# GpSimd's tables for the second layer, issued behind a gate in the first MLP

## The chip, the cores and the metric

The kernel runs on one core of a Trainium2 chip. The core has five engines that run side by side, each with its own in-order queue: TensorE (PE, with its weight loads as PEld), VectorE (DVE), ScalarE (ACT), GpSimd (POOL) and SyncE (SP), which here only issues DMAs. The metric is the device time of one execution in microseconds (us), the median of several runs. All data is float32.

## The reference

Two decoder layers on a residual of 512 tokens by 1024 channels. Each layer projects the normed residual once, feeds three mixers (sparse attention, an S5 state space, a Mamba-2 SSD), projects their outputs back, and then applies an MLP of width 4096:

```python
for l in range(DEPTH):                      # DEPTH = 2
    h = _rmsnorm(x, norm_mix_g[l])
    z = h @ w_in[l]
    q, k, v, qi, ki, wi, u5, z_ssd, xbc, dt_raw = _split(z, IN_SIZES)
    attn_out = _dsa_mixer(q, k, v, qi, ki, wi, attn_q_norm_g[l], ..., cos, sin)
    s5_out = _s5_mixer(u5, s5_lambda_re[l], s5_lambda_im[l], s5_log_step[l],
                       s5_b_re[l], s5_b_im[l], s5_c_re[l], s5_c_im[l], ...)
    ssd_out = _ssd_mixer(z_ssd, xbc, dt_raw, ...)
    mix = jnp.concatenate([attn_out, s5_out, ssd_out], axis=-1) @ w_out[l]
    x = x + mix
    h2 = _rmsnorm(x, norm_mlp_g[l])
    x = x + ((jax.nn.relu(h2 @ w_up[l]) ** 2) @ w_down[l])
```

What the change moves are tables that depend on parameters alone and not on x: for S5 the discretised input matrices, their powers, the rotations of each chunk and a short convolution kernel, and for attention the rotary tables with the gains of the norms folded in. The set for the second layer can be made at any time before that layer's mixers read it.

## The kernel before

**Matrix products.** Every large product runs as three matmuls of hi and lo parts (lines 436 to 438, psum tile `pm`). The class `Slabs` brings the weights: a slab of 128 x 512 is loaded by SP (`wraw`), its high part `whi` is made by ACT (L171), and its low part `wlo` by DVE (L172). Slabs are requested and split three and one ahead in the code, with 3 buffers for `wraw` and 5 for `whi` and `wlo`.

**Stages.** A layer is `mixers(l)` and then `mlp(l)`. The mixers are some eight generators (the W_in slices, keys, top-k selection L1076 and L1077, attention, S5, SSD, the out projection) that `merge` traces side by side. The MLP walks four quarters of the hidden width, each as four pairs of up tiles (relu squared: ACT L1381, DVE L1384, ACT L1385, DVE L1386) and four pairs of down tiles (DVE L1392, and L1393 into the residual `x`).

**Tables.** `s5_tables(l)` makes S5's tables. For the second layer all its elementwise work is on POOL: `bb` (L589 to L594), the products in the helper `outer` (L604 to L606) for `s5b`, `BPp` and later `CA`, the rotations `COS` and `SIN` (L630 to L640), a sign on `s5bc` (L645), and for the convolution kernel `strip` (L660, L661) and a cleared `M` (L663). Between them PE transposes `BPp` (`s5B`, L618) and multiplies `CA` (`s5st`, L653), and SP copies `strip` into `M` (L666). `rope_tables(l)` makes `ropec`, `ropeq`, `ropes` and `ropeg` on POOL (L955 to L966). For the first layer both stand in the mixers; for the second they are the generator `prepare(1)`, which `run` merges with `mlp(0)`, so in the text they come during the first MLP.

**What sets the order.** The text is not the order. A scheduler takes every traced instruction with a priority (its place in the trace) and with what it depends on, and puts on each engine's queue, in its own model of time, the most urgent instruction that is ready. The second layer's tables depend on nothing late, so on POOL, which has little else to do, they are taken as soon as their buffers are free, long before their place in the text; what needs a buffer of the mixers (`ropec`) or a PE result (`CA` onward) comes later.

Of the kernel before, what the change touches and what calls it, by code (L numbers as in the profile page):

```python
# [21 lines left out]
L = 2  # L22
NB = S // P          # token blocks
KC = D // P          # channel chunks of the trunk
# [8 lines left out]
T5 = 8               # tokens of one S5 chunk  # L33
C5 = S // T5         # S5 chunks
G5 = 16
GBUFS = {"g": 52, "t": 16}
BANKS = {"m": 4, "a": 4}    # PSUM banks: trunk, attention, S5 and SSD
EARLY = 2           # slabs loaded along with x
S5_ON_DVE = True
CONV_ON_ACT = False  # L40
# how the streams of work of a layer's mixers are laid side by side: the order of W_in's slices, the blocks whose
# selections run side by side, the parts of the out projection, which of S5 and SSD waits for the other, each
# stream's pace and delay, and the banks
# [41 lines left out]
WB = (3, 5)    # weight slabs in flight: as loaded, and split  # L85
OUTER = {"tok": True, "chan": True}    # products slab by slab
AHEAD = (3, 1)    # slabs requested and split ahead of the one in use

# columns of the packed per-partition parameters
# [18 lines left out]
# constants  # L108
# [8 lines left out]
# W_in slices: (first column, width), in the host's column order  # L117
# [17 lines left out]
class Slabs:  # L135
    """slabs of weight matrices in the order of their use: loaded and split into hi and lo parts some way ahead"""
# [9 lines left out]
    def turn(self, key):  # L146
        """whether the slabs before these have been used up"""
        return self.i == self.starts[key]
# [32 lines left out]
    def take(self, n, tiles, outer):  # L181
        """the next n slabs for each of some tiles, as (tile, slab number, hi, lo): slab by slab if outer, else
        tile by tile, and then those to follow are split while the last tile uses these up"""
        if outer:
            for j in range(n):
                hi, lo = self.next()[0]
                for t in range(tiles):
                    yield t, j, hi, lo
            return
        cur = []  # L190
        for t in range(tiles):
            for j in range(n):
                if t == 0:
                    cur += self.next()
                elif t == tiles - 1:
                    self.load(self.i + AHEAD[0] + j)
                    self.split(self.i + AHEAD[1] + j)
                yield t, j, cur[j][0], cur[j][1]


class Net:
    def __init__(self, ctx, tc, a, taps=None):
# [11 lines left out]
        self.uid = 0  # L214

# [9 lines left out]
    def h(self, shape=(P, 512), dt=F32, name="h"):  # L225
        """as g, for S5 and SSD"""
        return self.g(shape, dt, name, "h")

    def tt(self, shape=(P, 512), dt=F32, name="t"):
        """as g, for the matrices of S5"""  # L230
        return self.g(shape, dt, name, "t")

    def small(self, n, tag="g"):
        """[P, n] tiles for what one stretch of small instructions needs, cut from one slot"""
# [59 lines left out]
    def rsqrt(self, y, x, n, eng=None):  # L294
        """y = 1/sqrt(x), [P, n] small"""
# [11 lines left out]
    def stt(self, v, out, x, s, y, op0, op1):  # L307
        """out = (x op0 s) op1 y, [P, n] small; GpSimd takes two instructions for it"""
# [7 lines left out]
    def expacc(self, out, x, t, v):  # L316
        """out = exp(x) to about an ulp, [P, n] small"""
# [15 lines left out]
    def sincos(self, c, s, th, t, v):  # L333
        """c, s = cos(th), sin(th), [P, n] small"""
# [14 lines left out]
        self.stt(v, q, q, 1.0, r, ALU.add, ALU.mult)      # sin(th/2)  # L349
# [4 lines left out]
        # cos(th/2) = 1 + w  # L354
# [9 lines left out]
    def norm_chunk(self, c, squares=True):  # L364
        """hi and lo parts of x*g, and the sum of squares over channels (still per partition)"""
# [25 lines left out]
    def token_sums(self, acc, perm=False):  # L391
        """[P, 4]: mean square + eps per token; block b is tokens b*128 + m, or with perm 4m + 3-b"""
# [10 lines left out]
    def bcast_tokens(self, colv, k):  # L403
        """[P, 4] per-token columns -> psum tile [P, 512] with the token's value on every partition"""
# [6 lines left out]
    def add_slabs(self, l):  # L411
        """the weights of a layer, in the order of their use"""
# [20 lines left out]
    def mm3(self, p, lh, ll, rh, rl, first, last):  # L433
        """p += (lh+ll)^T (rh+rl), without the product of the two low parts (below float32's last bit)"""
# [5 lines left out]
    def gemm_tok(self, ps, xh, xl, slabs, sls):  # L440
        """token-major blocks: psum tile of block i [tok, n] = ps(i), tokens sls[i]; yields (cost, finished tile)"""
# [14 lines left out]
    def gemm_chan(self, ps, slabs, xh, xl):  # L456
        """channel-major tiles of 128 columns of a slice of 256: [chan, tok]; yields (cost, finished tile)"""
# [13 lines left out]
    def s5_small(self):  # L471
        """powers of the discretised state matrix and the input matrices, both layers"""
# [38 lines left out]
        # powers 0..8  # L511
# [17 lines left out]
        # X = (pr; pi), Y = (-pi; pr) on the two halves of the partitions  # L529
# [8 lines left out]
        # m8 and the rotation of one chunk, with the angle's sign turned on the lower half  # L538
# [4 lines left out]
        self.rot = []          # e^{+-i phi 2^k}  # L543
# [22 lines left out]
    def s5_tables(self, l, t):  # L566
        """the matrices of one layer's chunked recurrence, into t"""
# [29 lines left out]
        def outer(v, out, u, w, u2, w2, gs, d0, d1):  # L597
            """out[g, d, h] = u[g, h] w[g, d] + u2[g, h] w2[g, d]"""
# [9 lines left out]
        for q in range(4):  # L608
# [4 lines left out]
            BPp = self.tt([P, 4, 8, 16], name="BPp")               # d = 1..8: the states stand one step ahead  # L613
            outer(v, BPp, bbr, X, bbi, Y, gs, 1, 9)
            # transposed input powers: rows (d, h')
# [8 lines left out]
        # rotations by chunk  # L624
# [21 lines left out]
        for q in range(4):  # L646
            v = eng(f"C{q}")
            gs = slice(4 * q, 4 * q + 4)
            ca = self.tt([P, 4, 8, 16], name="CA")                 # d = 0..7
# [7 lines left out]
            # the skip term joins the kernel's first tap  # L657
# [14 lines left out]
    def s5(self, l, tab, usb, out):  # L672
        """usb: token-major input -> hi/lo of the two channel-major output tiles"""
# [5 lines left out]
        # input with rows (d = 7-i, h')  # L679
# [48 lines left out]
        # rows (half of the groups, chunk)  # L728
# [16 lines left out]
        # channel-major, columns (token of the chunk, half, chunk)  # L745
        gg = []
        for jh in range(2):
# [8 lines left out]
            v.scalar_tensor_tensor(t, t, 1.0, p, ALU.add, ALU.mult)      # 2 gelu(y)  # L756
# [25 lines left out]
    def ssd(self, l, r_, out):  # L782
# [3 lines left out]
        # step sizes  # L786
# [37 lines left out]
        # convolution and silu, each with half the argument  # L824
        xc = {}
        for m in (0, 1, 2, 3) if self.plan["w_order"].index("xa") < self.plan["w_order"].index("xb") else (2, 3, 0, 1):
# [16 lines left out]
            else:  # L843
                # C of each group, with zeros on the other group's partitions
# [8 lines left out]
        for b in range(NB):  # L853
            bs = slice(b * P, (b + 1) * P)
            # the sums of a dt up to each token of the block, on every partition
# [10 lines left out]
            # token-major inputs  # L866
# [12 lines left out]
            # scores  # L879
# [33 lines left out]
        # gate and group norm  # L913
# [30 lines left out]
    def rope_tables(self, l):  # L944
        """gains folded into the rotation, c and s for (k, k, ki) and for the rotated part of q; the gains of the rest of
        q stand in those of k"""
        nc = self.nc
        v = nc.gpsimd
        cos = self.tab_("cos").rearrange("p (b e) -> p b e", b=NB)     # (cos | cos)
        sin = self.tab_("sin").rearrange("p (b e) -> p b e", b=NB)     # (-sin | sin)  # L950
# [18 lines left out]
    def head_ms(self, out, src, nh):  # L969
        """mean square over the 64 of each head, + eps"""  # L970
# [6 lines left out]
    def rope(self, x, rs, c, s):  # L977
        """x = rope(x * rs * gain), of the keys"""
# [8 lines left out]
    def rope_q(self, x, c, s):  # L987
        """the rotated part of eight heads' queries"""
# [8 lines left out]
    def attn_keys(self, l, ksb, rt):  # L997
        """ksb: [P, 3, 64] per block (k0 k1 ki): norm, rope, transposes"""
# [7 lines left out]
        # hi and lo parts of the keys, each on both halves of the partitions  # L1006
# [18 lines left out]
    def transpose_heads(self, src):  # L1025
        """[P, 8, 64] token-major -> per head [P (hi d, lo d), P tokens]"""
# [15 lines left out]
    def head_dot(self, p, q, K, i, nk):  # L1042
        """p[tok, key] = q . k, both with all of their bits"""
# [3 lines left out]
    def index_scores(self, b, qi, K, wi, accs):  # L1047
        """masked scores of block b (>= 1): [P, (b+1)*128]"""
# [21 lines left out]
    def topk_masks(self, accs):  # L1070
        """the 128 largest of each row (lowest index first among equals) keep 0, the rest get NEG"""
# [10 lines left out]
    def attend(self, b, qT, K, mask, nrs, ah, al):  # L1082
        """nrs: minus the scale of each head's logits"""
# [42 lines left out]
    def merge(self, name, streams):  # L1126
        """trace several streams of work side by side: in a given order, or each at its own pace"""
# [4 lines left out]
        def step(i):  # L1132
            if i not in live:
                return True
            self.tc.cur_priority -= prio[i]
            try:
                c = next(gens[i])
# [7 lines left out]
        while live:  # L1145
            for i in sorted(live, key=lambda i: clock[i]):
# [6 lines left out]
                # blocked: it resumes no earlier than the others stand  # L1153
# [3 lines left out]
    def trunk_in(self, l, r):  # L1157
        """the slices of W_in"""
# [17 lines left out]
        def done(k, i, p):  # L1176
            """the finished tile i of a slice out of its bank"""
            if k == "u5":
                if "usb" not in r:
                    # S5 input, tokens 8c + 4e + 3-b at row (c, e) of block b  # L1180
# [7 lines left out]
            elif k[0] in "xz":  # L1188
                # SSD inputs, channel-major
# [11 lines left out]
            else:  # L1201
# [6 lines left out]
                else:  # L1208
                    t = self.g([P, NH, 64], name=k)            # the queries in pairs (r, 4+r)
# [11 lines left out]
        if l == 0:  # L1221
            # the first two slices side by side, as the channels of x come in
# [27 lines left out]
        for k in order:  # L1250
# [7 lines left out]
            else:  # L1258
                # every key of the first block is kept: no scores
# [81 lines left out]
    def out_proj(self, l, mix, part):  # L1341
        """x += (the chunks of some of the mixers) @ (their rows of w_out)"""
# [19 lines left out]
    def mlp(self, l):  # L1362
# [10 lines left out]
        nc.scalar.activation(rb, self.bcast_tokens(r2, "a"), AF.Copy)  # L1373
        for q, up, j in plan:
# [27 lines left out]
    def prepare(self, l):  # L1402
        """what the next layer's mixers need of their parameters"""
# [22 lines left out]
    def run(self, stop=None):  # L1426
        self.tc.cur_priority = 100000
        self.load()
        for l in range(L):
# [6 lines left out]
            if l + 1 < L:  # L1436
                streams.append((self.prepare(l + 1), 0.0))
# [96 lines left out]
```

## Time and profile before

| | us |
|---|---|
| runs | 1361.53, 1359.96, 1359.14 |
| median | 1359.96 |
| span of the profiled execution | 1356.7 |
| PE busy | 1247.9 (92%) |
| DVE busy | 883.2 (65%) |
| ACT busy | 564.6 (42%) |
| POOL busy | 161.6 (12%) |

All stretches below are in us from the start of the span. The first layer's mixers run to about 362, the first MLP follows up to some 600 us, and then the second layer's stages. L12 is line 12 of the kernel before. POOL's own busy time is small over the whole, and most of it lies in the first 250 us. A row of the timeline gives the start, the duration, what ran, and in brackets how long the engine had been idle and what released it. A row of the windows gives a stretch, its length, and for each engine the busy time and the number of instructions. A duration includes any time in which the instruction, once begun, is held up.

### The profile page before, as it was taken

How to read it: one execution, taken by the hardware profiler on the slowest of the kernel's cores; microseconds unless marked ns; L12 is line 12 of the kernel's file. 1: busy time of each engine (PE TensorE's matmuls, PEld its weight loads, DVE VectorE, ACT ScalarE, POOL GpSimd, SP SyncE). 2: the span in 40 equal slices, each digit the busy share in tenths (PEclk: the TensorE clock that was granted, in tenths of full speed). 3: DMA queues.
4: the chain of work that ended last, by engine and by line, in shares of the span. 5: the costliest groups of instructions: out<-in, count | busy, mean ns of one | idle time of the engine just before them, and what ended most of it. 6: DMA issues, size and time to landing. Idle time of an engine off the chain costs nothing. (4 is left out here: it accounts for less than half of the span.)

```text
span 1356.7 us, 17071 instructions
## 1 busy us (share of the span) xinstructions
PE 1247.9 (92%) x5852; PEld 1013.6 (75%) x5852; DVE 883.2 (65%) x2044; ACT 564.6 (42%) x1160; POOL 161.6 (12%) x301
## 2 busy tenths in 40 slices
PE   6679966879999999999999998978999999999998
PEld 5667854647888877888888897755688888888887
DVE  6899799884844544444466779998575444445443
ACT  4346352563542332423444535656454233242331
POOL 2593268200000221000000000000000000000000
PEclk9789987899999999999999998989999999999999
DMA  6122120001233323323323312100123333333332
GB/s 193 47 78 71 25 68 11 32 1 47 86 95 100 94 83 94 101 96 99 94 84 89 100 31 53 63 16 16 35 83 102 95 99 94 101 94 101 93 108 86
DMA packets 102694, 103.74 MB, mean 76 GB/s; under 512 B 10960, under 2 KB 95696, under 8 KB 102608
## 3 DMA queue, kind: packets, MB, share of 16 engines
q1 hardware_dynamic: 102608, 102.66, 25.1%
q8 instruction: 46, 0.75, 0.2%
q14 instruction: 40, 0.33, 0.1%
HBM read 99.36 MB, written 2.10 MB: 75 GB/s over the span
## 5 line engine op out<-in xcount | busy, mean ns | idle before, releaser
L172 DVE TENSOR_TENSOR wlo<-wraw,whi 128x512 fp32r<-128x512 f32 (+1 forms) x368 | 253.8, 691 | 300.6 <-ACT whi L171 298.4
L171 ACT ACTIVATE whi<-wraw 128x512 fp32r<-128x512 f32 (+1 forms) x368 | 229.0, 624 | 498.5 <-PE pm L437 332.4
L436 PE MATMUL pm<-xh,whi 128*128 128x512 f32 x608 | 239.8, 395 | 2.7 <-ACT usb L1186 1.1
L437 PE MATMUL pm<-xl,whi 128*128 128x512 f32 x608 | 238.5, 393 | 0.0
L438 PE MATMUL pm<-xh,wlo 128*128 128x512 f32 x608 | 238.4, 393 | 0.0
L438 PE MATMUL pm<-uh,wlo 128*128 128x512 f32 x512 | 199.5, 390 | 1.2 <-DVE wlo L172 1.2
L437 PE MATMUL pm<-ul,whi 128*128 128x512 f32 x512 | 199.7, 390 | 0.0
L436 PE MATMUL pm<-uh,whi 128*128 128x512 f32 x512 | 199.6, 390 | 0.0
L436 PEld LDWEIGHTS pm<-xh,whi 128*128 128x128 f32 x608 | 115.2, 190 | 27.6 <-ACT q L1210 1.6
L438 PEld LDWEIGHTS pm<-xh,wlo 128*128 128x128 f32 x608 | 115.1, 189 | 24.4 <-issue 0.3
L437 PEld LDWEIGHTS pm<-xl,whi 128*128 128x128 f32 x608 | 115.3, 190 | 23.1 <-DVE xl L372 0.2
L438 PEld LDWEIGHTS pm<-uh,wlo 128*128 128x128 f32 x512 | 96.2, 188 | 21.7 <-DVE wlo L172 1.6
L436 PE MATMUL pm<-whi,xh 128*128 128x512 f32 (+2 forms) x240 | 94.1, 395 | 19.8 <-ACT xh L370 12.4
L437 PEld LDWEIGHTS pm<-ul,whi 128*128 128x128 f32 x512 | 96.2, 188 | 20.3 <-issue 0.4
L436 PEld LDWEIGHTS pm<-uh,whi 128*128 128x128 f32 x512 | 96.2, 188 | 19.9 <-issue 0.2
L437 PE MATMUL pm<-wlo,xh 128*128 128x512 f32 (+2 forms) x240 | 92.5, 386 | 2.3 <-DVE wlo L172 2.3
L438 PE MATMUL pm<-whi,xl 128*128 128x512 f32 (+2 forms) x240 | 92.2, 388 | 1.5 <-DVE xl L372 1.4
L436 PEld LDWEIGHTS pm<-whi,xh 128*128 128x128 f32 x240 | 55.9, 234 | 27.1 <-ACT xh L370 12.8
L437 PEld LDWEIGHTS pm<-wlo,xh 128*128 128x128 f32 x240 | 56.3, 235 | 7.6 <-DVE wlo L172 3.4
L438 PEld LDWEIGHTS pm<-whi,xl 128*128 128x128 f32 x240 | 55.7, 234 | 7.1 <-DVE xl L372 2.5
L1384 DVE SCALAR_TENSOR_TENSOR ur<-pm,ur 128x512 f32<-128x512 f32 x64 | 44.0, 687 | 25.5 <-ACT ur L1381 25.5
L1392 DVE TENSOR_TENSOR sq<-pm,r2b 128x512 f32<-128x512 f32 x64 | 44.2, 690 | 23.2 <-PE pm L438 23.2
(349 smaller groups left out, 1915.2 us busy)
## 6 DMA issues: line engine op xcount, KB each, us to landing
wraw<-in_w_up_dram SPq DMA_DIRECT2D x128, 256.0 KB, 2.7
wraw<-in_w_down_dram SPq DMA_DIRECT2D x128, 256.0 KB, 2.7
wraw<-in_w_in_dram SPq DMA_DIRECT2D x64, 256.0 KB, 2.7
wraw<-in_w_out_dram SPq DMA_DIRECT2D x32, 256.0 KB, 2.7
wraw<-in_w_in_dram SPq DMA_DIRECT2D x16, 166.0 KB, 2.3
x<-in_xT_dram SPq DMA_DIRECT2D x8, 256.0 KB, 5.9
out_dram<-x SPq DMA_DIRECT2D x8, 256.0 KB, 2.0
s5bc<-in_s5bc_dram SPq DMA_DIRECT2D x4, 256.0 KB, 4.7
```

What stands on the lines that cost most here:

```text
L171: nc.scalar.activation(hi, raw, AF.Copy)
L172: nc.vector.tensor_tensor(lo, raw, hi.bitcast(F32), ALU.subtract)
L436: nc.tensor.matmul(p, lh, rh, start=first, stop=False)
L437: nc.tensor.matmul(p, lh, rl, start=False, stop=False)
L438: nc.tensor.matmul(p, ll, rh, start=False, stop=last)
L1384: v.scalar_tensor_tensor(r, p, 0.0, r, ALU.max, ALU.mult)
L1392: v.tensor_tensor(t, d[1], rb, ALU.mult)
```

## The change

`mlp(0)` now also issues one small POOL copy, the gate, of `r2`, which is the reciprocal of the norm's mean square that opens the MLP (L1371 before). Each step of `prepare(1)` is traced under `issue_after` the gate: POOL instructions that it traces may not be put ahead of the gate in POOL's queue. Nothing is removed, and apart from the copy nothing is added; the work on other engines that `prepare(1)` traces keeps its place.

```diff
         r2 = self.s([P, 4], tag="r2", bufs=1)
         v.reciprocal(r2, ms)
         rb = self.g(name="r2b")
         nc.scalar.activation(rb, self.bcast_tokens(r2, "a"), AF.Copy)
+        if l + 1 < L:
+            self.gate = nc.gpsimd.tensor_copy(self.s([P, 4], tag="gate", bufs=1), r2)
         for q, up, j in plan:
...
             self.tc.cur_priority -= prio[i]
+            held = len(streams[i]) > 2 and streams[i][2] == "prep"
             try:
-                c = next(gens[i])
+                with self.tc.issue_after(self.gate.ins) if held and self.gate else nullcontext():
+                    c = next(gens[i])
...
             if l + 1 < L:
-                streams.append((self.prepare(l + 1), 0.0))
+                streams.append((self.prepare(l + 1), 0.0, "prep"))
```

The orders of DVE, ACT and SP are those of before, and PE's too but for two neighbouring matmuls late in the program; only POOL's changes. In the rows below names are as in the program, a number behind a name is the scheduler's count of buffers, and lines of the kernel after stand one higher up to L966 and a few higher behind.

The first place is POOL in the middle of the first mixers, at 111 to 137 us of the trace, where it makes the first layer's `CA`. Before:

```order
L605 TENSOR_TENSOR pt_1669<-s5bc_109,s5Y 128x512
L660 TENSOR_TENSOR pt_1680<-cons,s5dd_112 16x64
L606 TENSOR_TENSOR CA_1668<-CA_1668,pt_1669 128x512
L605 TENSOR_TENSOR pt_1780<-s5bc_109,s5Y 128x512
L965 TENSOR_TENSOR ropes_5055<-cols,rows 128x4x8
L966 TENSOR_TENSOR ropes_5055<-cols,rows 128x4x8
```

After:

```order
L606 TENSOR_TENSOR pt_1669<-s5bc_109,s5Y 128x512
L661 TENSOR_TENSOR pt_1680<-cons,s5dd_112 16x64
L607 TENSOR_TENSOR CA_1668<-CA_1668,pt_1669 128x512
L606 TENSOR_TENSOR pt_1780<-s5bc_109,s5Y 128x512
L664 MEMSET M_399_1683 128x512
L605 TENSOR_TENSOR CA_1779<-s5bc_109,s5X 128x512
```

Before, the second layer's rope tables (eight rows of `ropes` and one of `ropeq`) stand ahead of the first layer's next `M` and `CA`; now these follow at once, and the rope rows stand behind the gate.

The second place is POOL where the first layer's tables end and the second layer's begin, at 175 to 193 us of the trace. Before (`CA_2145`, `M_507` and `strip_2155` are the last of the first layer; `bb_4590`, `s5b_1109` and `BPp_4604` belong to the second):

```order
L604 TENSOR_TENSOR CA_2145<-s5bc_109,s5X 128x512
L606 TENSOR_TENSOR CA_2145<-CA_2145,pt_2146 128x512
L590 TENSOR_TENSOR pt_4591<-s5bc_4584,s5ci 128x256
L645 TENSOR_SCALAR s5bc_4585<-s5bc_4585,cols 128x512
L663 MEMSET M_507_2160 128x512
L589 TENSOR_TENSOR bb_4590<-s5bc_4584,s5cr 128x256
L661 TENSOR_TENSOR strip_2155<-strip_2155,pt_2157 16x4x16
L593 TENSOR_TENSOR bb_4590<-s5bc_4584,s5cr 128x256
L591 TENSOR_TENSOR bb_4590<-bb_4590,pt_4591 128x256
L594 TENSOR_TENSOR pt_4595<-s5bc_4584,s5ci 128x256
L604 TENSOR_TENSOR s5b_1109_4599<-bb_4590,s5X 128x64
L604 TENSOR_TENSOR BPp_4604<-bb_4590,s5X 128x512
```

After:

```order
L605 TENSOR_TENSOR CA_2145<-s5bc_109,s5X 128x512
L607 TENSOR_TENSOR CA_2145<-CA_2145,pt_2146 128x512
L664 MEMSET M_507_2160 128x512
L662 TENSOR_TENSOR strip_2155<-strip_2155,pt_2157 16x4x16
L1379 COPY gate_3598<-r_885_3589 128x4
L590 TENSOR_TENSOR bb_4592<-s5bc_4586,s5cr 128x256
L591 TENSOR_TENSOR pt_4593<-s5bc_4586,s5ci 128x256
L594 TENSOR_TENSOR bb_4592<-s5bc_4586,s5cr 128x256
L592 TENSOR_TENSOR bb_4592<-bb_4592,pt_4593 128x256
L595 TENSOR_TENSOR pt_4597<-s5bc_4586,s5ci 128x256
L605 TENSOR_TENSOR s5b_1110_4601<-bb_4592,s5X 128x64
L605 TENSOR_TENSOR BPp_4606<-bb_4592,s5X 128x512
```

The second layer's tables ran straight on from the first layer's and between them; now the gate stands between the two, and everything behind it waits for the reciprocal in the MLP. From the first `COS` of the second layer onward POOL's order is the same in both.

## Rows read from the trace of the kernel before

**Rows 1.** The page: busy time, share and instructions of each engine.

```profile
PE 1247.9 (92%) x5852; PEld 1013.6 (75%) x5852; DVE 883.2 (65%) x2044; ACT 564.6 (42%) x1160; POOL 161.6 (12%) x301
```

**Rows 2.** Windows: start:end, length, PE, PEld, DVE, ACT, POOL, PEclk, DMA share, GB/s.

```profile
190.00:246.00 56.00, 34.24 (x165) 26.23 (x163) 53.59 (x103) 15.87 (x32) 51.62 (x105) 0.82 0.07 19
380.00:440.00 60.00, 60.00 (x266) 49.74 (x265) 28.41 (x43) 18.76 (x32) 0.83 (x3) 1.00 0.32 97
439.00:449.00 10.00, 10.00 (x46) 8.29 (x45) 7.12 (x8) 2.53 (x4) 8.83 (x17) 1.00 0.34 104
```

**Rows 3.** Timeline of PE in the first mixers: start, us, what, idle before and releaser.

```profile
194.54 0.47 PE L739 MATMUL s5y<-CA,X 128*64 128x128 f32 x2 [4.23 <-DVE X L726]
...
206.73 0.48 PE L739 MATMUL s5y<-CA,X 128*64 128x128 f32 x1 [6.72 <-DVE X L726]
```

**Rows 4.** Timeline of DVE in the same stretch, S5's chunk rotations and scans.

```profile
184.92 1.98 DVE L720 TENSOR_TENSOR_SCAN sw<-s5m,sv 128x64 f32<-128x64 f32 x8
...
189.45 2.65 DVE L716 TENSOR_TENSOR sv<-sv,svs 128x512 f32<-128x512 f32 x1
192.02 2.46 DVE L726 TENSOR_TENSOR X<-sw,sws 128x504 f32<-128x504 f32 x1
194.41 5.66 DVE L720 TENSOR_TENSOR_SCAN sw<-s5m,sv 128x64 f32<-128x64 f32 x8
...
201.47 1.52 DVE L724 TENSOR_TENSOR sw<-sw,COS 128x512 f32<-128x512 f32 x1
...
203.00 1.45 DVE L725 TENSOR_TENSOR sws<-sws,SIN 128x512 f32<-128x512 f32 x1
204.37 1.72 DVE L1107 TENSOR_SCALAR pe<-pe,psum 128x128 f32<-128x128 f32 x3
```

**Rows 5.** Same DVE lines where POOL is idle: second layer (ns min/median/max), one earlier.

```profile
L716 DVE TENSOR_TENSOR sv<-sv,svs x2: 682/684/685, 827.7 to 833.8; 128x512 f32<-128x512 f32 x2
...
L726 DVE TENSOR_TENSOR X<-sw,sws x2: 675/676/678, 834.4 to 839.7; 128x504 f32<-128x504 f32 x2
...
L724 DVE TENSOR_TENSOR sw<-sw,COS x2: 692/692/693, 832.6 to 837.9; 128x512 f32<-128x512 f32 x2
...
L725 DVE TENSOR_TENSOR sws<-sws,SIN x2: 684/684/685, 833.2 to 838.5; 128x512 f32<-128x512 f32 x2
...
155.58 0.67 DVE L1107 TENSOR_SCALAR pe<-pe,psum 128x128 f32<-128x128 f32 x3
```

**Rows 6.** POOL's timeline around the first and the second layer's tables.

```profile
132.30 0.25 POOL L965 TENSOR_TENSOR ropes<-cols,rows 128x32 f32<-128x32 f32 x1 [20.53 <-DVE rsw L993]
...
181.70 2.35 POOL L645 TENSOR_SCALAR s5bc<-s5bc,cols 128x512 f32<-128x512 f32 x1 [7.59 <-DMA s5bc<-in_s5bc_dram]
...
190.26 0.71 POOL L591 TENSOR_TENSOR bb<-bb,pt 128x256 f32<-128x256 f32 x1
...
213.04 0.12 POOL L630 MEMSET COS<- 128x8 f32 x1
...
439.17 0.25 POOL L961 TENSOR_TENSOR ropec<-cols,rows 128x32 f32<-128x32 f32 x1 [192.35 <-PE pm L438]
...
482.45 1.06 POOL L604 TENSOR_TENSOR CA<-s5bc,s5X 128x512 f32<-128x512 f32 x1 [34.45 <-PE s5B L618]
```

**Rows 7.** Later DVE lines beside POOL's tables, 189 to 248, then line 1033 later.

```profile
L769 DVE SCALAR_TENSOR_TENSOR sig<-sig,ge x4: 405/632/837, 223.8 to 228.0; 128x256 f32<-128x256 f32 x4
...
L1033 DVE TENSOR_TENSOR hhl<-q,hhl x2: 937/958/979, 243.5 to 246.2; 128x256 fp32r<-128x256 f32 x2
...
L1033 DVE TENSOR_TENSOR hhl<-q,hhl x8: 400/418/426, 866.7 to 937.0; 128x256 fp32r<-128x256 f32 x8
```

**Rows 8.** The first MLP: its opening norm, a slab's low part, and that line beside POOL.

```profile
362.58 0.17 DVE L1371 RECIPROCAL r<-ms 128x4 f32<-128x4 f32 x1
...
375.01 0.69 DVE L172 TENSOR_TENSOR wlo<-wraw,whi 128x512 fp32r<-128x512 f32 x1 [2.03 <-ACT whi L171]
...
L172 DVE TENSOR_TENSOR wlo<-wraw,whi 128x512 fp32r<-128x512 f32 x4 | 3.8, 944 | 3.6 <-ACT whi L171 3.6
```

More of the change, by code (lines that the diff above doesn't have):

```diff
@@ L1 @@
 import math
-from contextlib import ExitStack
+from contextlib import ExitStack, nullcontext
 import numpy as np
@@ L214, in __init__ @@
         self.uid = 0
+        self.gate = None
     def nm(self, s):
```

## The prediction, made before the changed kernel ran

> **What bounds the kernel now.** I read the page first. PE is busy 92% of the span and POOL 12% [rows 1], so over the whole, PE is the bound and POOL cannot matter. That average hides the stage that the change touches, so I read the windows next [rows 2]. From 190 to 246 us, in the first mixers, DVE is busy 53.59 of 56 us, PE only 34.24, at a granted clock of 0.82, and POOL 51.62. There DVE is the bound. From 380 to 440 us, in the first MLP, PE is busy 60.00 of 60 us at full clock, DVE needs 28.41, and POOL is idle. There PE is the bound and DVE has half its time free.
>
> Then PE's timeline in the first stretch: PE stands 4.23 and 6.72 us, both times until DVE has written `X` [rows 3]. So what DVE does just before those two instants sets the end of the stage. DVE's timeline shows what: single instructions of 1.45 to 5.66 us [rows 4]. The same forms in the second layer, where POOL does nothing, take 0.68 us [rows 5]. And POOL's timeline shows what runs beside them: from 181.70 us on, its instructions follow one another until 439.17 - 192.35 = 246.82 us [rows 6], and by the names in the order from about 185 on nearly all are the second layer's tables.
>
> **What the change takes away: DVE's slowed instructions.** I go through the slowed ones in order, each against the same form without POOL [rows 4, 5]; for the eight scans I take the eight just before, 1.98 us.
> - L716: 2.65 - 0.68 = 1.97
> - L726: 2.46 - 0.67 = 1.79
> - eight of L720: 5.66 - 1.98 = 3.68
> - L724: 1.52 - 0.69 = 0.83
> - L725: 1.45 - 0.68 = 0.77
> - three of L1107: 1.72 - 0.67 = 1.05
>
> The sum is 10.1 us. It lies between 189.45 and 204.37 + 1.72 = 206.09 us, a stretch of 16.6 us; so without POOL the same work takes 6.5 us, and DVE ran here at 6.5 / 16.6 = 39% of its speed. All of it stands ahead of an `X` on which PE waits, so it should come off the path whole, as long as nothing else is late by less than 10 us.
>
> After 206 us POOL goes on, with smaller instructions. The two groups that I can price: four of L769 at a mean of 632 ns where the fastest took 405, 0.9 us; two of L1033 at 958 where the second layer has 418, 1.1 us [rows 7]. That is 2.0 us more, 12.1 in all. I take 11: the first 10.1 and about half of the rest, since between 206 and 246 the work also passes through PE and ACT and not every instruction of DVE is waited for. The 80 or so DVE instructions there that I did not price may hold as much again as the 2.0, so the upper end of the gain is 14.6 with the 0.5 below.
>
> A rule of the Trainium skill names a cause. The page "SBUF — State Buffer", section "Who interferes with whom", says that VectorE and GpSimd share one pair of ports under an exclusive lock: whoever issues first has it for the whole instruction and the other stands, where the VectorE instruction has two inputs in SBUF and the GpSimd one reads SBUF. Nearly all the forms slowed above fit it in kind, but not in size: read as one lock for each instruction, L716 would lose at most one POOL instruction, about 0.71 us [rows 6], and it lost 1.97. By that reading the six lines above would hold some 0.7 us for each of 15 instructions at most, which is 10.5, and the sum would stay. The same section speaks against the change: the lock goes with the work to wherever the tables are made, and VectorE's `wlo` also has two SBUF inputs.
>
> **What it moves: the tables into the MLP.** Behind the gate POOL has 246.82 - 181.70 = 65 us of tables and a few us of rope rows, starting when the reciprocal is done, at 362.58 us [rows 8] in before's time. DVE will be slowed there. It needs 28.41 of 60 us, 47% [rows 2]. The wide instructions of the tables, which slowed it to 39%, last from 181.70 to 213.04 us [rows 6], 31 us. In those 31 us DVE falls behind by (0.47 - 0.39) x 31 = 2.4 us, and then catches up. Against that stands its lead: `whi` and `wlo` have five buffers, one in use and four ahead; a slab feeds 12 matmuls at 60.00 / 266 = 0.226 us each [rows 2], so four slabs are 10.8 us, less the 0.69 of a `wlo` and about as much for its `whi`: 9.5 us. DVE's idle time before a `wlo` ends with ACT's `whi` [rows 8], so DVE itself is not late now. The direct evidence is the one place where POOL already works in the MLP: from 439 to 449 us POOL is busy 8.83 of 10 us, `wlo` takes 944 ns on average in place of 690, and PE is busy 10.00 of 10 [rows 2, 8]. I take a cost of 0, by that row, and keep 0 to 2.4 as its bounds.
>
> **The wait that it adds.** The gate stands in POOL's queue, and behind it stand only the second layer's tables, then `ropec` and `CA`. Who waits for these: `ropec` got its buffer at 439.17, and `CA` waited 34.45 us for PE's `s5B` until 482.45 [rows 6]. Tables made from 363 on are done at about 363 + 65 + 4 = 432, 7 us before the first and 50 before the second. `s5B` stands in PE's queue where it stood, and so do the DMAs of `s5bc` and of `strip` in SP's: a DMA that waits for tables finds them done. Nothing is queued behind the gate that the first layer needs; its last `M` and `strip` now stand just ahead of it. The copy itself is 128 x 4 and lies in POOL's free time: 0.
>
> **What it moves for the first layer.** `ropes` kept POOL standing for 20.53 us until 132.30 [rows 6], waiting for DVE to release it, with the first layer's `CA` behind. These go up to 20 us earlier. PE is not shown waiting for them, and where they overlap DVE they slow it earlier by as much as they now slow it later: I take 0, with 0.5 either way.
>
> **The sum.** 11.0 + 0 - 0 = 11.0 off the profiled span of 1356.7, so 1345.7. The median of the runs, 1359.96, lies 3.3 above that span; the same on top gives **1349.0**.
>
> **Rivals.**
> - *Part of the gain is caught by another wait.* Ahead of the same matmuls stand ACT's evictions and the `strip` DMAs, and behind 206 us a chain through PE and ACT. If these are late by half, 3 to 8 us are left, 5.5 in the middle: 1354.5. For it: PE runs there at 0.82 of its clock and is itself busy 34 of 56 us [rows 2]. Against it: both waits of PE name DVE's `X`, and DVE is busy 96% of the stretch.
> - *Nothing happens.* DVE's slow instructions would be slow for another reason than POOL, or the MLP takes back what the mixers give: 1360. For it: I argue from overlap alone. Against it: the second layer runs the same forms, on the same shapes, at a quarter of the time.
> - *Slower: POOL keeps DVE out in the MLP.* The mechanism is the same slowing, in the stage where PE is the bound. At no progress at all for 65 us DVE would fall back by 0.47 x 65 = 31 us; 9.5 are covered, 21 land on PE, less the 11 won: 1370. It decides from the point where 9.5 + 11 = 20.5 of the 31 us are lost, a progress of DVE of 16% of full speed throughout. The worst single row is 0.68 of 2.65, 26% [rows 4, 5], and a slowed DVE has 53% of its time to spare.
>
> By the skill's rule read literally, the MLP's instructions from PSUM (L1384, L1392) would not be touched and only those with two SBUF inputs would; the backlog would be smaller than the 2.4 above, and the time the same 1349.0.
>
> **How the numbers follow.** Forecast, a gain of 9 to 14.6: 0.64, with 0.02 above that. Part of it: 0.22. Nothing: 0.07. Slower: 0.05. 0.2% of the median is 2.7 us, about what a measurement of this kernel can tell from no change; the first two cases lie beyond it. So faster is 0.88, same 0.07, slower 0.05. The low end is 1360.0 - 14.6 = 1345.4. The high end goes into the second case as far as a gain of 4.5, 1355.5: that leaves out a third of that case, both others and the 0.02, some 2 in 10.
>
> **What would show it.** In the profile after: POOL idle from about 175 us to the MLP, then busy some 65 us; the lines of rows 4 at 0.68 us, or 2 us for eight scans, between 185 and 200; PE's two waits for `X` gone or under 2 us; the MLP beginning about 11 us earlier; `wlo` at 0.9 to 1.5 us in the first part of the MLP with PE still busy 60 of 60. The prediction is wrong in its first step if those lines are fast and the MLP begins no earlier (another wait came due), and in its second if PE stands before L438 or L436 for `wlo` in the MLP. If `s5B` or `ropec` is late, POOL took far longer than 65 us beside DVE.

## The result, and the profile after

The changed kernel took 1345.42 us (median of 1344.43 to 1347.79) against 1359.55 us for the kernel before, of which there are four runs now: a ratio of 0.9897, 95% interval 0.9882 to 0.9912, so 14.1 us less. Run four times more, against 21 runs of the kernel before, it took 1347.55 us, ratio 0.9905 (0.9892 to 0.9919). The prediction was 1349.0 us in a range of 1345.4 to 1355.5: a gain of 11, where 12 to 14 came.

The windows of the first mixers and of the first MLP after the change (start:end, length, PE, PEld, DVE, ACT, POOL, PEclk, DMA share, GB/s):

```profile
190.00:246.00 56.00, 40.54 (x214) 30.48 (x213) 52.44 (x142) 25.00 (x61) 0.00 (x0) 0.85 0.12 37
...
360.00:420.00 60.00, 60.00 (x266) 49.73 (x265) 38.51 (x46) 20.30 (x34) 54.28 (x104) 1.00 0.31 97
```

Against [rows 2]: POOL does nothing any more in this stretch of the first mixers, where it was busy 51.62 us, and DVE does more in the same 56 us, 142 instructions for 103. In the MLP POOL is now busy 54.28 of 60 us, DVE is busy 38.51 us with 46 instructions, where 46 took 30.30 us from 374 to 434 us before the change, and PE is still busy 60.00 of 60.

PE's two waits for `X` are nearly gone (timeline: start, us, what, idle before and releaser), against 4.23 and 6.72 us in [rows 3]. The third row is what follows on `s5y`:

```profile
190.90 0.43 PE L740 MATMUL s5y<-CA,X 128*64 128x128 f32 x2 [0.18 <-DVE X L727]
...
196.31 0.32 PE L740 MATMUL s5y<-CA,X 128*64 128x128 f32 x1 [1.48 <-DVE X L727]
...
200.28 1.09 PE L751 MATMUL s5yT<-cons,ysb 128*128 128x128 f32 x8 [0.47 <-ACT ysb L744]
```

The same row before the change:

```profile
213.19 1.09 PE L750 MATMUL s5yT<-cons,ysb 128*128 128x128 f32 x8 [0.47 <-ACT ysb L743]
```

DVE's timeline ahead of the second `X`, against [rows 4] (lines one higher):

```profile
189.44 0.81 DVE L717 TENSOR_TENSOR sv<-sv,svs 128x512 f32<-128x512 f32 x1
190.18 0.67 DVE L727 TENSOR_TENSOR X<-sw,sws 128x504 f32<-128x504 f32 x1
190.77 1.55 DVE L721 TENSOR_TENSOR_SCAN sw<-s5m,sv 128x64 f32<-128x64 f32 x8
...
193.72 0.69 DVE L725 TENSOR_TENSOR sw<-sw,COS 128x512 f32<-128x512 f32 x1
...
194.42 0.66 DVE L726 TENSOR_TENSOR sws<-sws,SIN 128x512 f32<-128x512 f32 x1
194.99 0.67 DVE L1108 TENSOR_SCALAR pe<-pe,psum 128x128 f32<-128x128 f32 x3
195.58 0.67 DVE L727 TENSOR_TENSOR X<-sw,sws 128x504 f32<-128x504 f32 x1
...
348.71 0.17 DVE L1374 RECIPROCAL r<-ms 128x4 f32<-128x4 f32 x1
```

As far as the second `X` it is the same list of instructions from the same starting time, 189.44 against 189.45, and it is through 10.4 us earlier.

POOL's timeline after, against [rows 6]: the first layer's last `strip`, the gate, the last of the rotation tables, `ropec` and the first late `CA`:

```profile
188.88 0.81 POOL L662 TENSOR_TENSOR strip<-strip,pt 16x64 f32<-16x64 f32 x1 [8.74 <-ACT strip L657]
...
348.94 0.56 POOL L1379 COPY gate<-r 128x4 f32<-128x4 f32 x1 [159.24 <-DVE r L1374]
...
417.32 1.12 POOL L641 TENSOR_TENSOR SIN<-pt,pt 128x256 f32<-128x256 f32 x1
425.30 0.25 POOL L962 TENSOR_TENSOR ropec<-cols,rows 128x32 f32<-128x32 f32 x1 [6.87 <-PE pm L439]
...
468.58 1.06 POOL L605 TENSOR_TENSOR CA<-s5bc,s5X 128x512 f32<-128x512 f32 x1 [34.45 <-PE s5B L619]
```

The gate stood 159 us, and nobody waited for what is behind it: `ropec` is again held by its buffer and `CA` by PE, for the same 34.45 us as before.

Where the gain was made, from the two profiles:

| point | before | after | ahead by |
|---|---|---|---|
| first s5y behind the second `X` (PE) | 206.73 | 196.31 | 10.4 |
| first s5yT, behind s5y (PE) | 213.19 | 200.28 | 12.9 |
| reciprocal that opens the first MLP (DVE) | 362.58 | 348.71 | 13.9 |
| `ropec` in the first MLP (POOL) | 439.17 | 425.30 | 13.9 |
| end of the span | 1356.7 | 1346.0 | 10.7 |

The last line is scatter between executions, not the change. The 3.2 us went in the second layer's mixers, where the two programs do the same: in the stretch from 945 to 968 us of before, and 930 to 957 of after, the granted clock was 0.93 and 0.81. From a reciprocal early in those mixers (L800, L801 after) to the one that opens the second MLP, the kernel before took 255.5 us here and 259.4 when profiled once more (below), and the changed kernel 258.7 and 257.4.

### The profile page after: what moved, and what is told of

It is laid out like the page before. It is cut to its first block, busy times and chain, and to the rows that moved or that the text cites. A ratio compares the mean times of both kernels' runs of the same rounds, so it can differ in the third digit from the quotient of the medians.

```text
span 1346.0 us, 17073 instructions
## 1 busy us (share of the span) xinstructions
PE 1245.8 (93%) x5852; PEld 1008.7 (75%) x5852; DVE 881.0 (65%) x2044; ACT 565.1 (42%) x1160; POOL 165.8 (12%) x302
## 5 line engine op out<-in xcount | busy, mean ns | idle before, releaser
L172 DVE TENSOR_TENSOR wlo<-wraw,whi 128x512 fp32r<-128x512 f32 (+1 forms) x368 | 260.5, 710 | 290.6 <-ACT whi L171 289.6
L437 PE MATMUL pm<-whi,xh 128*128 128x512 f32 (+2 forms) x240 | 92.9, 390 | 19.8 <-ACT xh L371 12.2
L1392 DVE TENSOR_TENSOR ul<-ur,uh 128x512 fp32r<-128x512 f32 x64 | 47.0, 735 | 22.4 <-ACT uh L1391 22.4
L1390 DVE SCALAR_TENSOR_TENSOR ur<-pm,ur 128x512 f32<-128x512 f32 x64 | 43.9, 686 | 24.3 <-ACT ur L1387 24.3
```

What stands on the lines that cost most here:

```text
L172: nc.vector.tensor_tensor(lo, raw, hi.bitcast(F32), ALU.subtract)
L437: nc.tensor.matmul(p, lh, rh, start=first, stop=False)
L1390: v.scalar_tensor_tensor(r, p, 0.0, r, ALU.max, ALU.mult)
L1392: v.tensor_tensor(lo, r, h.bitcast(F32), ALU.subtract)
```

## The experiments

Theory A: GpSimd's instructions on S5's tables slow VectorE's instructions ahead of `X`, and nothing else of the change matters. Rival B: the gain is that GpSimd no longer stands 20 us ahead of the first layer's `CA` for `ropes`. Theory C: a share of the gain is TensorE's clock, which fell during the long wait. And for the MLP: VectorE, slowed there in turn, has lead enough, against: it has not.

**The changed kernel again, and the kernel before again.** Nothing is edited.

> The changed kernel once more, with more rounds, for a narrower ratio and a second profile. The first profile was 13.9 us ahead of before at the end of the first MLP but only 10.7 at the end: 3.2 us went in the second layer's mixers, where the granted clock was low for 10.2 us where before had 3.4. If that was the state of one execution: 1345 to 1346, ratio 0.9895 to 0.9905, and this profile keeps some 13 to 14 us to the end. If the change itself causes it: the same low clock at the same place, and a span near 1346 again.

> The kernel before once more, for a second profile. In eight profiles of other kernels the second layer's mixers lose some 2 us, against the first profile of before, in a stretch at low granted clock near its 947 to 957 us. If the first profile of before was lucky there: the loss shows here too, and the span is 1357.5 to 1358.5. If the changes cause it: no loss, a span near 1356.7. If s5y at half clock belongs to the long wait for X: s5y behind the second X takes 6 to 6.5 us again.

The changed kernel: 1347.55 us, ratio 0.9905 (0.9892 to 0.9919), above the 1345 to 1346 that I expected; span 1344.5, 12.2 us ahead of the first profile of before and not 13 to 14. The kernel before against itself: 1.0006 (0.9996 to 1.0015), span 1361.3, 4.6 us longer than in its first profile and longer than expected; 3.8 of these it lost in the second layer's mixers. So single executions of this one kernel differ by more than the 3.2 us, which are scatter. Both executions of the kernel before have the long waits and the slow s5y.

**Each half alone.** First with the rope tables left free, then with only them gated:

```diff
-        self.gate = None
+        self.gate, self.loose = None, False
...
-            held = len(streams[i]) > 2 and streams[i][2] == "prep"
+            held = len(streams[i]) > 2 and streams[i][2] == "prep" and not self.loose
...
         yield from self.s5_tables(l, self.tab)
+        self.loose = True
+        yield 0.0
         self.rt = self.rope_tables(l)
```

> Only the S5 tables are behind the gate; the rope tables stand in the first mixers as before. Theory A (the S5 tables' wide instructions on GpSimd slow VectorE ahead of X): the whole gain stays, 1345 to 1347. Rival B (the gain is that GpSimd no longer stands 20 us ahead of the first layer's CA, for the rope tables): most of it is gone, 1355 to 1360.

1345.64 us, ratio 0.9895 (0.9880 to 0.9910). GpSimd stands 20.54 us for `ropes` as before, and the whole gain is there. Rival B is out.

```diff
         yield from self.s5_tables(l, self.tab)
-        self.rt = self.rope_tables(l)
+        with self.tc.issue_after(self.gate.ins):
+            self.rt = self.rope_tables(l)
...
-                streams.append((self.prepare(l + 1), 0.0, "prep"))
+                streams.append((self.prepare(l + 1), 0.0))
```

> The other half: only the rope tables are behind the gate, the S5 tables run in the first mixers. Theory A: no gain, or the tables start up to 20 us earlier and collide with other VectorE work, 1357 to 1362. Rival B: 1345 to 1349.

1357.36 us, ratio 0.9978 (0.9969 to 0.9987): a small gain that neither theory had. Its POOL timeline tells why:

```profile
203.22 1.53 POOL L606 TENSOR_TENSOR pt<-bb,s5Y 128x512 f32<-128x512 f32 x1
360.16 0.56 POOL L1379 COPY gate<-r 128x4 f32<-128x4 f32 x1 [155.41 <-DVE r L1374]
```

A queue is in order. The scheduler put the gate into the middle of S5's tables, and what stands behind it waited too, gated or not: POOL fell silent at 204.75 us. So this run did not test the rope tables by themselves. What it shows instead, if the rope tables bring nothing, is the price of S5's tables from 204.75 us on: 3.0 us (1.8 to 4.2). About 1.8 of them lie ahead of `X`, whose last instructions ran at full speed: PE's wait for it was 4.86 us, not 6.72.

**GpSimd work of another kind in the tables' place.** Behind the first layer's last `strip`, in the changed kernel, instructions that nobody needs; with n = 45 and 12 products of two operands in SBUF, and with 100 memsets:

```diff
-            pool.tensor_tensor(strip[:, :, 0], strip[:, :, 0], d, ALU.add)
+            last = pool.tensor_tensor(strip[:, :, 0], strip[:, :, 0], d, ALU.add)
+            if l == 0 and q == 3:
+                junk = self.cp.tile([P, 512], F32, name="junk")
+                here = self.tc.cur_priority
+                with self.tc.issue_after(last.ins):
+                    for _ in range(n):
+                        pool.tensor_tensor(junk, self.cons[:, :512], self.cons[:, :512], ALU.mult)
+                self.tc.cur_priority = here
```

> The changed kernel with 45 extra GpSimd instructions right behind the first layer's last strip, in the place in which the second layer's tables stood: products of two 128x512 operands in SBUF into a tile that nobody reads, about 45 to 60 us of GpSimd time from 189 us on. Theory A (any GpSimd instructions that read SBUF slow VectorE there): VectorE's lines ahead of X take 2 to 3 times their time again, X is 8 to 12 us late, and the time is 1356 to 1362. Rival (it was something else in the tables, their DMAs or their buffers): 1344 to 1347.

> The changed kernel with only 12 of the extra GpSimd products behind the first layer's last strip, about 15 us from 189 us on, done when X is. It prices what is lost ahead of X alone. VectorE's instructions there lose about one GpSimd instruction of 1.1 to 1.3 us each, X is 8 to 10 us late, and if TensorE's clock falls again in s5y behind the long wait, 2 us more: 1355 to 1358. If the delay of X is caught later in the mixers: 1346 to 1350.

> The same with 100 memsets of 128x512, about 52 us of GpSimd time that only writes SBUF. By the rule that only a GpSimd instruction that reads SBUF takes the ports from VectorE's second operand: VectorE's lines stay at 0.68 us, 1344 to 1347. If writing alone also slows it: X late and 1350 to 1360.

45 products: 1364.04 us, ratio to before 1.0029 (1.0018 to 1.0040); the whole gain is lost and more, beyond the 1356 to 1362 that I expected. 12 products: 1356.76 us, 0.9985 (0.9975 to 0.9995). Its rows, DVE, POOL and PE:

```profile
190.61 1.81 DVE L724 TENSOR_TENSOR sv<-sv,svs 128x512 f32<-128x512 f32 x1
...
193.78 4.79 DVE L728 TENSOR_TENSOR_SCAN sw<-s5m,sv 128x64 f32<-128x64 f32 x8
...
190.84 15.53 POOL L668 TENSOR_TENSOR junk<-cons 128x512 f32<-128x512 f32 x12
...
207.09 0.47 PE L747 MATMUL s5y<-CA,X 128*64 128x128 f32 x1 [9.23 <-DVE X L734]
```

POOL works for 15.5 us and is done at 206.4, just when `X` is; `X` is some 10 us later than in the changed kernel, and the kernel loses 9 to 12 us against the two measurements of the changed kernel. So a delay of `X` passes to the end nearly one for one, as the prediction took it, and it needs no table, no table's DMA and no table's buffer. The other 33 products of the first run, all beside what comes behind `X`, cost 6 to 7 us more. 100 memsets, 59 us of GpSimd time in the same place: 1346.71 us, 0.9902 (0.9889 to 0.9915), no cost. Its DVE groups from 186 to 197 us (instructions, busy us, mean ns):

```profile
L728 DVE TENSOR_TENSOR_SCAN sw<-s5m,sv 128x64 f32<-128x64 f32 x13 | 2.5, 261 | 0.0
L732 DVE TENSOR_TENSOR sw<-sw,COS 128x512 f32<-128x512 f32 x2 | 1.4, 693 | 0.1
...
L1115 DVE TENSOR_SCALAR pe<-pe,psum 128x128 f32<-128x128 f32 x3 | 1.1, 493 | 0.0
```

Here only the last form is slower beside memsets (1.1 us for three, 0.7 without), and in the rest of the 59 us other TENSOR_SCALARs of its kind (six of 128x256 at 622 ns, 347 without). So not GpSimd's being busy matters, but what it does: the forms with two inputs in SBUF were slow beside products, which read SBUF, and are not beside memsets, which only write it.

**The tables beside the rest of the mixers.** The gate copies four columns of the second `X` in place of `r2`:

```diff
+            if l == 0 and hf == 1:
+                here = self.tc.cur_priority
+                self.gate = nc.gpsimd.tensor_copy(self.s([P, 4], tag="gate", bufs=1), X[hf][:, 0, 1:5])
+                self.tc.cur_priority = here
...
-            self.gate = nc.gpsimd.tensor_copy(self.s([P, 4], tag="gate", bufs=1), r2)
+            pass
```

> The changed kernel with the gate not on the norm of the MLP but on the second X of the first layer, so that the tables run from about 197 to 262 us beside the rest of the first mixers. It prices what the tables cost behind X alone, which the prediction put at 2.0 us for two groups of lines and at up to 4.0 with what was not priced. By that: 1347 to 1350. If only the instructions ahead of X matter: 1345 to 1347. If the rest of the mixers is as sensitive: 1354 to 1358.

1350.55 us, 0.9941 (0.9928 to 0.9954): by the ratios 5 to 6 us more than the changed kernel. That is just above the first expectation, 1347 to 1350, and below the third. PE's wait for `pT` behind `glu` and attention is 8.31 us there and 5.59 in the changed kernel:

```profile
221.51 2.45 PE L1123 MATMUL po<-pT,vt 128*64 128x512 f32 x4 [8.31 <-ACT pT L1120]
```

So the same tables cost some four tenths of the price behind `X`: DVE is the bound there too, but much of its work is the top-k selection, MAX8 at 543 and MATCH_REPLACE8 at 535 ns for 128x384, as fast beside the tables as without them (549 and 541).

**TensorE's clock.** In the kernel before, 20 matmuls that nobody needs, on a part of `p` that is overwritten later:

```diff
+                    if (l, q, j, hf) == (0, 0, 0, 1):
+                        here = self.tc.cur_priority
+                        self.tc.cur_priority += 1000
+                        for _ in range(20):
+                            nc.tensor.matmul(p[:, P:2 * P], self.ident, X[0][:, 0:2].rearrange("p g c -> p (g c)"), start=True, stop=True)
+                        self.tc.cur_priority = here
```

> The kernel before, with 20 extra matmuls of 128 columns on a part of a psum bank that is overwritten later, 15 of them in the time in which PE waits 6.7 us for the second X; VectorE's and GpSimd's slowness there stays. In before the matmuls s5y behind that wait ran at half clock and took 6.5 us, after the change 4.0. Theory C (a share of some 2.5 us of the gain is TensorE's clock, which fell in the long wait): s5y behind the wait takes about 4.0 to 4.5 us in place of 6.5, and the median falls by about 2 us. Against it: s5y still takes 6 us or more, the time stays within 1 us of before.

1360.46 us, 1.0003 (0.9993 to 1.0012): no gain. Its two windows, the wait and the s5y behind it, and the row of PE between the two:

```profile
201.30:207.50 6.20, 3.96 (x34) 3.56 (x32) 6.20 (x12) 2.33 (x6) 5.89 (x6) 0.99 0.26 85
207.50:214.30 6.80, 6.47 (x64) 5.78 (x64) 6.80 (x21) 0.65 (x2) 6.56 (x11) 0.76 0.13 39
```

```profile
207.53 0.47 PE L745 MATMUL s5y<-CA,X 128*64 128x128 f32 x1 [2.27 <-DVE X L726]
```

PE was busy 3.96 of 6.2 us in the wait, at a granted clock of 0.99, and then stood 2.27 us for `X` all the same; s5y (with five of the extra matmuls among it) still had only 0.76. The order of some DVE instructions behind it changed as well. So this run does not support C in the form in which it was expected, and does not exclude that a wait filled to the end would help; that was not tried.

**What the MLP bears.** In the second MLP, where GpSimd is idle, n = 30 and 240 of the products behind the reciprocal:

```diff
+        if l + 1 == L:
+            pool, here = nc.gpsimd, self.tc.cur_priority
+            gate = pool.tensor_copy(self.s([P, 4], tag="gate", bufs=1), r2)
+            junk = self.s([P, 512], tag="junk", bufs=1)
+            with self.tc.issue_after(gate.ins):
+                for _ in range(n):
+                    pool.tensor_tensor(junk, self.cons[:, :512], self.cons[:, :512], ALU.mult)
+            self.tc.cur_priority = here
```

> The changed kernel with 30 of these products on GpSimd behind the reciprocal that opens the second MLP, where GpSimd has nothing else to do: some 32 to 45 us. It prices by itself what the tables cost in an MLP. My theory (VectorE falls behind by less than its lead of 9.5 us): no cost, within 1 us of the changed kernel. Rival: evictions on VectorE have less lead than wlo, and PE stands: 2 to 8 us more.

> The same with 240 products, 250 to 340 us, most of the second MLP. VectorE ran at 39% of its speed beside wide GpSimd instructions and needs 47%. If that holds here, it falls behind by (0.47 / 0.39 - 1) x 300 = some 60 us, of which 9.5 are covered: 1380 to 1400. If VectorE keeps half its speed or more, it never falls behind: 1344 to 1347.

30: 1347.86 us, 0.9911 (0.9897 to 0.9926). 240: 1346.38 us, 0.9902 (0.9889 to 0.9916). Neither differs from the changed kernel's 0.9897 and 0.9905. The window 1000 to 1100 us of the changed kernel and of the one with 240, then the latter's DVE groups from 1000 to 1200 us:

```profile
1000.00:1100.00 100.00, 100.00 (x449) 82.66 (x449) 49.97 (x79) 35.75 (x60) 0.00 (x0) 1.00 0.32 99
```

```profile
1000.00:1100.00 100.00, 100.00 (x450) 82.66 (x449) 79.75 (x79) 36.44 (x62) 90.24 (x71) 1.00 0.31 96
```

```profile
L172 DVE TENSOR_TENSOR wlo<-wraw,whi 128x512 fp32r<-128x512 f32 x74 | 91.8, 1254 | 28.0 <-ACT whi L171 27.4 <-PE pm L439 0.3
...
L1398 DVE SCALAR_TENSOR_TENSOR ur<-pm,ur 128x512 f32<-128x512 f32 x21 | 14.3, 682 | 2.5 <-ACT ur L1395 2.3
L1406 DVE TENSOR_TENSOR sq<-pm,r2b 128x512 f32<-128x512 f32 x16 | 10.9, 681 | 0.2 <-PE pm L439 0.2
```

With POOL busy 90 of 100 us, the same 79 instructions take DVE 79.75 us where they took 49.97: 63% of its speed, not 39%, and it needs 50%. So it does not fall behind in the 310 us that POOL goes on. `wlo` takes 1254 ns in place of 690, but the two forms that take their first operand from PSUM stay at 682 and 681 (688 and 691 in the changed kernel).

**A try at a faster kernel.** The first layer's second pair of rotation tables, moved behind a gate on the first top-k result:

```diff
+            while l == 0 and hf in (1,) and self.gate0 is None:
+                yield None
+            held = ExitStack()
+            if l == 0 and hf in (1,):
+                held.enter_context(self.tc.issue_after(self.gate0.ins))
             v = eng(f"R{hf}")
...
+            held.close()
...
+                if self.gate0 is None:
+                    here = self.tc.cur_priority
+                    self.gate0 = self.nc.gpsimd.tensor_copy(self.s([P, 4], tag="gate0", bufs=1), m8[:, :4])
+                    self.tc.cur_priority = here
```

> A try at a faster kernel: the changed kernel with, in addition, the first layer's second pair of rotation tables behind a gate on the first result of the top-k selection, so that GpSimd makes them beside VectorE's MAX8 and MATCH_REPLACE8, which have one operand, and not beside the index scores, where wlo takes 891 ns and the scores 927. The order of the other engines changes too, since S5's tables are traced later. If VectorE's slowed instructions at 88 to 107 us are on the path: 1340 to 1344. If S5's tables then come too late for X: 1348 to 1360.

1363.70 us, 1.0033 (1.0020 to 1.0046): the second expectation, and above its 1348 to 1360. The tables of the first layer have a reader soon, and everything of S5 behind them came late; PE's timeline:

```profile
204.32 1.11 PE L1043 MATMUL hTp<-cons,hhl 128*128 128x128 f32 x4 [11.14 <-DVE hhl L1040]
...
228.00 0.70 PE L745 MATMUL s5y<-M,U 128*64 128x128 f32 x4 [2.65 <-DMA M<-strip]
```

s5y begins at 223.40 us, when the changed kernel is long through with it, and `s5yT` behind it at 237.28 where the changed kernel has 200.28. Since the order of the other engines changed with it, the run does not say what the slowed instructions at 88 to 107 us cost.

## Why the prediction was right, and where it was off

- **The bound and the cause were right.** DVE ahead of `X` was the bound, and GpSimd's tables slowed it. The predicted 10.1 us is 10.4 in the profile; 12 GpSimd products without any table take 9 to 12 us of the gain back, and gating S5's tables alone gives the whole gain. The 0.3 us between come from a wrong base: the eight scans that I took as undisturbed, 1.98 us, were slowed themselves; after the change the same eight take 1.56 and the eight behind them 1.55. And "a quarter of the time", which I held against the rival of no gain, is true of L716 and L726 (26 and 27%); without POOL L724, L725 and L1107 take 39 to 47% of their time beside it.
- **The term behind `X` was too small.** I put about half of 2.0 us there; 3.5 came (13.9 - 10.4). The part from DVE is as priced: the four of L769 and the L1033 are back at 412 and 424 ns (medians), and from s5yT on the kernel gains 1.0 us. The other 2.5 us lie in s5y itself, a stretch of PE work that I took as fixed. The windows over it, before and after:

```profile
206.70:213.20 6.50, 5.99 (x55) 5.75 (x55) 6.38 (x19) 1.10 (x4) 6.26 (x10) 0.60 0.14 40
```

```profile
196.30:200.30 4.00, 3.51 (x55) 3.27 (x55) 4.00 (x15) 1.12 (x4) 0.00 (x0) 1.00 0.55 186
```

  The same 55 matmuls took 6.5 us at a granted clock of 0.60, which is four fifths of the time at the lower level of 1.2 GHz, and 4.0 us at 1.00, all at 2.4 GHz. Ahead of it PE had been busy 6.78 of 17.70 us before the change, and 8.65 of 10.30 after. The second profile of the kernel before has 0.60 again, the run with only the rope tables gated 0.70 behind a wait of 4.86 us, those with 12 and 45 products 0.71 and 0.72 behind waits of 9.23 and 9.25. The seven profiles in which PE waits under 2 us for either `X` have 1.00. (The last try, `later_cos`, where PE stands elsewhere, has 0.51.) That the low level goes with the long waits is shown by these rows; that the waits cause it is not, since filling one of them by two thirds did not undo it, and the longest ones have not the lowest clock. A stage behind a wait should have been priced at both levels of the clock.
- **The cost in the MLP was right at 0, its bound came from a wrong mix.** I carried the 39% over from instructions that nearly all have two operands in SBUF. In the MLP a quarter of DVE's time is L1390 and L1398 (before: L1384 and L1392), with one operand in PSUM. The first 33 us of the MLP after the change, DVE's groups:

```profile
L172 DVE TENSOR_TENSOR wlo<-wraw,whi 128x512 fp32r<-128x512 f32 x14 | 15.8, 1141 | 6.3 <-ACT whi L171 6.3
L1392 DVE TENSOR_TENSOR ul<-ur,uh 128x512 fp32r<-128x512 f32 x6 | 7.1, 1182 | 1.5 <-ACT uh L1391 1.4
L1390 DVE SCALAR_TENSOR_TENSOR ur<-pm,ur 128x512 f32<-128x512 f32 x6 | 4.1, 680 | 0.8 <-ACT ur L1387 0.8
```

  The forecast of `wlo` at 0.9 to 1.5 us with PE fully busy holds. The page "SBUF — State Buffer" of the Trainium skill, section "Who interferes with whom", has this split: VectorE contends where both inputs are in SBUF and GpSimd reads SBUF, and with one input there only in its 2-port modes. The trace agrees in three places: 680 ns beside the tables for the form from PSUM, 682 beside 240 products, and full speed beside memsets for the forms with two inputs in SBUF. The form that memsets did slow, a TENSOR_SCALAR, is of a kind that the same section counts among those that can take both ports of VectorE.
- **The slower rival fell with it.** It needed DVE at 16% of its speed for 65 us; the lowest measured over 100 us of an MLP is 63%, beside GpSimd work that goes on for 310 us.
- **The added wait cost nothing,** as worked out: the tables were done at 418.4 us, 14 us ahead of the 432 that I had put for a start at 363, since the MLP began 13.9 us earlier, and `ropec` waited 6.87 us for its buffer where I had put 7. That it fits so well is luck: my 65 us held 3.42 us in which POOL stood for the first layer's `strip`, and in the MLP the tables ran some 4 us longer, so that with the rope rows they took 68.98 us against the 69 that I had put.
- **The rope tables at 0** hold together with S5's: with and without them behind the gate the ratio is 0.9897 or 0.9905, and 0.9895. Alone they were not tested, as told above.
- **The way from span to median** took nothing from the forecast: 1349.0 is the median of before less 11.0, whatever lies between span and median. Of the 3.3 us that I added, 1.8 lie between the time and the span of any run of which both are known (1347.79 and 1346.0; 1363.13 and 1361.3), and the other 1.5 between the one profiled execution and the median.
- **The rival of a part gain** did not come: nothing else was late by less than 10 us.
- **That the first time lies in the range is luck in part.** It is 1345.42 against a low end of 1345.4. The range reached so far because I left up to 2.0 us for DVE instructions that I had not priced, and from s5yT on no more than 1.0 us came, priced ones and others together. The 2.5 us of the clock, which had no place in the sum or the range, filled that room.

## What to carry to other kernels

Work without a deadline on an engine that looks idle is not free: look at what its neighbour does beside it, instruction by instruction, and put it where the neighbour is not the bound. Price the same work in its new place by the forms that run there, not by those of the old place. And before gating one stream of work, look at what a scheduler puts behind the gate in the same queue.

## What the runs showed of the hardware that was not expected

- In the kernel before, L716 (189.45 to 192.10 us) lost 1.97 us beside GpSimd instructions of 0.81, 0.61, 0.71, 0.61 and 0.73 us (188.90 to 192.25 us), the third of them shown in [rows 6]; beside products of 1.29 us (310.1 us for 240) the same line lost 1.14. So a VectorE instruction can lose more than one short GpSimd instruction, but lost no more than one long one. The exclusive lock for each instruction, which the page "SBUF — State Buffer" of the Trainium skill states in "Who interferes with whom", does not explain the first; it stays open.
- Eight scans of 128x64, 1.55 us together, took 4.79 beside the products: each lost 0.4 us, a third of a product. They ran at 32% of their speed, where the 128x512 `sv` and the 128x504 `X` just ahead of them, at 1.81 and 1.51 us, ran at 38 and 44%. The short instructions lost the larger share.
